# Stick attention in rounds of two heads, attention's norm at eviction, and tokens transposed instead of multiplied with diagonals

## The chip, the cores and the metric

The kernel runs on one core of a Trainium2 chip. The metric is the device time of one launch in microseconds (us), as the median of several runs. The core has TensorE (PE; its weight loads are listed as PEld), VectorE (DVE), ScalarE (ACT), GpSimd (POOL) and SyncE (SP), which run side by side and wait for one another by semaphores; SP starts the loads of the large weights.

## The reference

256 tokens of width 1024 pass through two transformer layers. All is float32.

The first layer: `h = rms_norm(x) * (1 + scale1) + shift1`, where the shifts, scales and gates come from a small network on `c`. Then `proj = h @ w_in` feeds two mixers. The one is banded softmax attention with 8 heads of 64; its output of width 512 is normed over all heads together, `o_a = rms_norm(o_a, attn_out_gain)`, that is, each token is divided by its root mean square. The other is a gated delta rule with 4 heads of 128, `o_b`. Both together give `x = x + gate1 * (concat(o_a, o_b) @ w_out)`. Then `h2 = rms_norm(x) * (1 + scale2) + shift2` goes to PEER: queries `h2 @ w_query`, the best 16 of 128 x 128 experts for each of 8 heads, and `x = x + gate2 * y`.

The second layer: `proj = rms_norm(x) @ w_in_2` is cut into parts for HGRN2 (a gated linear recurrence with 8 heads), for stick-breaking attention with 16 heads of 64, and for two gates. Stick attention, for a block of 128 queries and all keys up to its end, with `z` the scores:

```
log_keep = where(key < query, log_sigmoid(-z), 0)
log_w = log_sigmoid(z) + cumsum(log_keep, reverse) - log_keep
a = where(key < query, exp(log_w), 0);  o = a @ v
```

`mixed = sigmoid(ga) * (o_hg @ w_hg) + sigmoid(gb) * (o_sb @ w_sb)`, `x = x + mixed @ w_o`, and a gated feed-forward layer ends it.

## The kernel before

Tokens lie on partitions in two tiles of 128 (`xt[:, i]`), or, for products that contract over features, transposed: `hT[:, k]` holds features 128k to 128k + 127 of all 256 tokens. Large products are made from two parts of each operand, `hi` (rounded by an ACT copy to float32r) and `lo` (the rest, a subtraction), as three products (`mm3`). Small products in float32 stand in the trace as two records each, a transpose as one. Nearly all rows bear line 237, the one where a helper counts each operation; so groups are told apart by tiles.

*The feeder* (lines 280 to 380) holds the list of weight units, 512 KB each. A unit is loaded by SP into `raw`, split into `whi` (ACT) and `wlo` (DVE, or POOL in some stages), up to three ahead, and multiplied in bursts of a few products. A unit has a gate: it can't start before its `hT` exists. Around it run *chains*, generators that make the mixers step by step. `drive` (line 438) decides in which order the program is written: it keeps an estimate of each engine's time and takes the next chain step when it is ready, else a burst of the feeder. Steps of chains are written with a higher priority (`urgent`), and the framework then orders each engine's instructions by its own simulation, priority and tokens; products that write one PSUM tile, or tiles given one token by `in_order`, keep their order among themselves. Of the 8 PSUM banks, 6 are `acc` and 2 are `tp`.

*Stage a* (line 1111) is the first layer's mixers. `attention_chain` (line 992) ends with the division by the softmax sum into `oa` (which lies in `qa`), then, lines 1079 to 1084, squares on ACT, `rsqrt` (three Newton steps on DVE) and a scaling of both token tiles. After that `split_T` (line 982) transposes `oa` and writes hi and lo into `mT[:, 0:4]`; the delta rule's output `ob` goes to `mT[:, 4:8]` after both of its token tiles are done. The output projection has four accumulators of 128 x 512 (two column halves n, two token tiles i), which stay open over attention's two units and the delta rule's two: `u0[0:2] + u1[0:2]`, later `u0[2:4] + u1[2:4]`. `add_mix` evicts each once: product with `gate1` into `mx_t`, sum into `xt`, squares for the next norm.

*Stage p* (line 1544) is PEER. It starts with `norm_T` (line 610): the sums of squares give `r = 1 / rms`, `norm_diag` makes two diagonal matrices with `r` (`nt_dg`), and `norm_part` (line 546) multiplies each 128 x 128 block of `xt` with one, which transposes and scales at once; DVE then applies scale and shift (`nt_full`), ACT and DVE write hi and lo. The query units start when the first tiles exist, and then the feeder fills PE.

*Stage b* (line 1921) is the second layer. `stick_chain` (line 1807) runs beside the projections of hg, ga, gb and the unit list of w_hg. w_sb's units come next and need its result `sbT`. A bank is 4 heads of equal parity r (the 64 rows r * 64 of `qT` and `kT`), one key block kt and one query block qt. There are 12 banks. `scores` makes `z` and from it on ACT, DVE, ACT, POOL the softplus in hi and lo (`sb_n`, `sb_nr`); `weights` adds the suffix sums to `z` in PSUM by products with `minus`, and takes the exponential (`sb_w`, or `sb_a` for the block 1, 1); `values` multiplies with v into 64 output partitions and evicts them. `sb_n` and `sb_w` take turns in two buffers. The steps are pipelined over banks: scores of bank s, values of bank s - 2, weights of bank s - 1.

## Time and profile before

| | us |
|---|---|
| median of 3 runs (1661.21 to 1662.28) | 1662.23 |
| profiled execution | 1660.82 |
| its span, first to last instruction | 1658.8 |
| PE busy in it | 1604.5 (97%) |
| DVE, ACT, POOL busy | 1094.6, 844.4, 337.3 |
| mean granted clock of PE | 0.988 |

Stage a ends at about 245 us, stage p runs to 1085, stage b to 1460, and the feed-forward layer ends the span. A row of the trace names engine, operation and tiles, `out<-in`; "idle before" is the time for which the engine had nothing to do ahead of an instruction, with what ended it. Matmuls are pipelined, so a record's length is more than the time from one to the next.

### The profile page before, as it was taken

The numbers are of one execution on the slowest core, as the hardware profiler recorded it, in microseconds if no ns is written. First come the engines' busy times: TensorE is split into PE (matmuls) and PEld (weight loads), VectorE is DVE, ScalarE is ACT, GpSimd is POOL, SyncE is SP. The second block draws the span as 40 slices with busy tenths as digits, with TensorE's granted clock in tenths as the row PEclk, the third lists the DMA queues.
The fourth block names the chain that finished last, engine by engine and source line by source line (L and its number), as shares of the span: only waits on it lengthen the run. The fifth ranks groups of instructions, "written<-read, shape, count | busy, mean of one in ns | idle before, by whom it ended". The sixth has DMA issues, their size and how long they took to land.

```text
span 1658.8 us, 28802 instructions
## 1 busy us (share of the span) xinstructions
PE 1604.5 (97%) x11336; PEld 1426.3 (86%) x11336; DVE 1094.6 (66%) x2034; ACT 844.4 (51%) x1314; POOL 337.3 (20%) x277
## 2 busy tenths in 40 slices
PE   7999979998999999999999999999999999999998
PEld 4878757888999999998888888889887898889997
DVE  3874765899967777874444444489886544656555
ACT  4553545654544444455544554465554866454443
POOL 0000001254323222242222222105322201000000
PEclk9999989999999999999999999999999999999999
DMA  8762335444555555556666666653444443546664
GB/s 331 253 218 102 126 110 195 145 153 150 172 164 165 166 166 166 166 166 191 193 195 195 190 193 195 196 155 118 147 125 130 139 141 115 167 141 189 186 185 138
DMA packets 77896, 279.36 MB, mean 168 GB/s; under 512 B 9664, under 2 KB 10048, under 8 KB 77632
## 3 DMA queue, kind: packets, MB, share of 16 engines
q1 hardware_dynamic: 71136, 257.72, 50.6%
q10 hardware_dynamic: 6624, 19.80, 3.6%
q8 instruction: 88, 1.44, 0.4%
q14 instruction: 48, 0.39, 0.1%
HBM read 276.44 MB, written 1.05 MB: 167 GB/s over the span
## 4 chain that ended last, share of the span: by engine, by line
PE 75%; DVE 7%; ACT 1%; issue 1%; POOL 1%; DMA 0%; DVEq 0%; ACTq 0%
PE acc L237 70%; PE tp L237 5%; DVE wlo L237 2%; DVE hg_Z L237 1%; DVE b_f L237 1%; DVE q_v L237 1%; DVE q_i L237 1%; DVE q_oh L237 0%; POOL wlo L237 0%; ACT whi L237 0%; POOL hg_Z L237 0%; DVE b_k L237 0%; DVE q_sc L237 0%; DVE xt L237 0%; ACT hg_Z L237 0%
## 5 line engine op out<-in xcount | busy, mean ns | idle before, releaser
L237 DVE TENSOR_TENSOR wlo<-raw,whi 128x1024 fp32r<-128x1024 f32 x415 | 517.7, 1249 | 371.9 <-ACT whi L237 370.8
L237 ACT ACTIVATE whi<-raw 128x1024 fp32r<-128x1024 f32 x470 | 495.2, 1055 | 407.2 <-PE acc L237 316.4
L237 PE MATMUL acc<-hT_hi,wlo 128*128 128x256 f32 x1728 | 492.8, 286 | 9.6 <-DVE wlo L237 7.8
L237 PE MATMUL acc<-hT_hi,whi 128*128 128x256 f32 x1728 | 494.4, 287 | 2.1 <-ACT whi L237 1.6
L237 PE MATMUL acc<-hT_lo,whi 128*128 128x256 f32 x1728 | 492.1, 285 | 1.3 <-DVE hT_lo L237 1.2
L237 PEld LDWEIGHTS acc<-hT_hi,wlo 128*128 128x128 f32 x1728 | 333.3, 193 | 13.6 <-DVE wlo L237 9.3
L237 PEld LDWEIGHTS acc<-hT_hi,whi 128*128 128x128 f32 x1728 | 333.0, 193 | 6.3 <-ACT whi L237 2.0
L237 PEld LDWEIGHTS acc<-hT_lo,whi 128*128 128x128 f32 x1728 | 333.4, 193 | 3.6 <-DVE hT_lo L237 1.9
L237 PE MATMUL acc<-wlo,hT_hi 128*128 128x512 f32 x832 | 328.1, 395 | 2.0 <-DVE wlo L237 2.0
L237 PE MATMUL acc<-whi,hT_lo 128*128 128x512 f32 x832 | 323.9, 391 | 0.0
L237 PE MATMUL acc<-whi,hT_hi 128*128 128x512 f32 x832 | 261.7, 394 | 0.9 <-ACT hT_hi L237 0.9
L237 POOL TENSOR_TENSOR wlo<-raw,whi 128x1024 fp32r<-128x1024 f32 x55 | 142.4, 2589 | 394.7 <-ACT whi L237 369.0
L237 PEld LDWEIGHTS acc<-wlo,hT_hi 128*128 128x128 f32 x832 | 156.4, 188 | 36.8 <-DVE wlo L237 2.6
L237 PEld LDWEIGHTS acc<-whi,hT_hi 128*128 128x128 f32 x832 | 156.0, 188 | 35.5 <-issue 3.1
L237 PEld LDWEIGHTS acc<-whi,hT_lo 128*128 128x128 f32 x832 | 156.4, 188 | 32.8 <-issue 0.8
L237 POOL TENSOR_TENSOR hT_lo<-A,hT_hi 128x256 fp32r<-128x256 f32 x128 | 97.4, 764 | 241.4 <-ACT hT_hi L237 241.4
L237 ACT ACTIVATE hT_hi<-A 128x256 fp32r<-128x256 f32 x128 | 52.8, 417 | 160.2 <-PE acc L237 160.2
L237 DVE TENSOR_TENSOR oh<-oh1e,c_g 128x512 f16<-128x512 f16 x128 | 75.0, 626 | 10.2 <-PE tp L237 9.5
L237 POOL TENSOR_TENSOR hg_Z<-b_k 128x512 f32<-128x512 f32 (+1 forms) x26 | 38.9, 1523 | 89.2 <-DVE b_k L237 41.9
L237 DVE SCALAR_TENSOR_TENSOR A<-tp,A 128x512 f32<-128x512 f32 (+26 forms) x52 | 28.4, 546 | 27.9 <-PE tp L237 27.8
L237 DVE TENSOR_TENSOR oh1e<-c_ih,iota 128x512 f16<-128x512 f16 x64 | 43.7, 683 | 0.9
L237 POOL TENSOR_TENSOR sb_nr<-sb_n,sb_nr 128x512 fp32r<-128x512 f32 x12 | 19.5, 1626 | 120.4 <-ACT sb_nr L237 120.4
(398 smaller groups left out, 1820.3 us busy)
## 6 DMA issues: line engine op xcount, KB each, us to landing
raw<-in_down SPq DMA_DIRECT2D x128, 512.0 KB, 3.6
raw<-in_up SPq DMA_DIRECT2D x128, 512.0 KB, 3.7
raw<-in_w_in SPq DMA_DIRECT2D x100, 512.0 KB, 3.7
raw<-in_w_ffn_in SPq DMA_DIRECT2D x44, 512.0 KB, 4.3
...
```

Source lines behind the costliest of these rows:

```text
L237: r = f(*args, **kw)
```

## The change

Three edits, and what they need:

- Stick attention goes by rounds: both parities r of 4 heads at a time, 6 rounds instead of 12 banks. Their score products alternate between the two 64-row halves, and their value products between the two halves of the output partitions, which are then evicted together. The order is now: weights of round s - 1, values of round s - 1, scores of round s.
- Attention's 1 / rms is no longer multiplied into `oa`. It is a column factor `ra` in an eviction of attention's part of the output projection, which has its own accumulators now (`tok_units` gets a first block `k0`); the delta rule's part has others, evicted later. `out_chain` transposes each token tile of `ob` as it is done. Attention's scores get a common token.
- `norm_part` scales 128 x 256 blocks of tokens, one on ACT and one on DVE, and transposes them.

```diff
@@ -473,25 +473,26 @@
     return tile
 
 
-def tok_units(g, w, grp, gate, post, ps_of=None, nk=NK):
+def tok_units(g, w, grp, gate, post, k0=0, nk=NK):
+
 
     nc, st = g.nc, []
 
     def unit(kq):
         def fn(wt):
             if kq == 0:
-                st.extend((ps_of or g.ps_acc).tile([128, 512], F32, name="acc") for _ in range(2))
+                st.extend(g.ps_acc.tile([128, 512], F32, name="acc") for _ in range(2))
             for kk in range(2):
                 k = kq * 2 + kk
                 for i in range(2):
-                    mm3(g, st[i], gate[0][:, k, i * 128:(i + 1) * 128], wt[:, kk], k == 0, k == nk - 1)
+                    mm3(g, st[i], gate[0][:, k0 + k, i * 128:(i + 1) * 128], wt[:, kk], k == 0, k == nk - 1)
                     yield
             if kq == nk // 2 - 1:
                 with urgent(g):
                     post(st)
         return fn
 
-    return [(w[grp, kq], (2, 512), unit(kq), gate) for kq in range(nk // 2)]
+    return [(w[grp, k0 // 2 + kq], (2, 512), unit(kq), gate) for kq in range(nk // 2)]
 
 
 def feat_units(g, w, grp, gate, post):
@@ -531,28 +532,37 @@
     g.nc.scalar.activation(junk, x, AF.Square, accum_out=ss)
 
 
+def norm_rms(g, pool, ss):
+
+    s2 = pool.tile([128, 2], F32, name="nt_s2")
+    g.nc.vector.tensor_tensor(s2, ss[:, :, 0], ss[:, :, 1], op=ALU.add)
+    return rsqrt(g, pool, s2, 2, 1.0 / D)
+
+
 def norm_diag(g, pool, ss):
 
-    nc = g.nc
-    s2 = pool.tile([128, 2], F32, name="nt_s2")
-    nc.vector.tensor_tensor(s2, ss[:, :, 0], ss[:, :, 1], op=ALU.add)
-    r = rsqrt(g, pool, s2, 2, 1.0 / D)
+    r = norm_rms(g, pool, ss)
     dg = pool.tile([128, 2, 128], F32, name="nt_dg")
     for i in range(2):
-        nc.vector.tensor_scalar(dg[:, i], g.c["ident"], r[:, i:i + 1], None, op0=ALU.mult)
+        g.nc.vector.tensor_scalar(dg[:, i], g.c["ident"], r[:, i:i + 1], None, op0=ALU.mult)
     return dg, r
 
 
-def norm_part(g, pool, xt, dg, hT, k, n, scale, shift):
-
+def norm_part(g, pool, xt, r, hT, k, scale, shift):
 
     nc = g.nc
-    ps = g.ps_t.tile([128, n, S], F32, name="tp")
-    for kk in range(n):
+    ps = g.ps_t.tile([128, 2, S], F32, name="tp")
+    xs = pool.tile([128, 2, 256], F32, name="nt_xs", tag="q_raw", bufs=8)
+    for i in range(2):
+        x = xt[:, i, k * 128:(k + 2) * 128]
+        if i:
+            nc.vector.tensor_scalar(xs[:, i], x, r[:, i:i + 1], None, op0=ALU.mult)
+        else:
+            nc.scalar.activation(xs[:, i], x, AF.Copy, scale=r[:, i:i + 1])
+    for kk in range(2):
         for i in range(2):
-            mm(g, ps[:, kk, i * 128:(i + 1) * 128], lhsT=xt[:, i, (k + kk) * 128:(k + kk + 1) * 128],
-                             rhs=dg[:, i])
-    for kk in range(n):
+            transpose(g, ps[:, kk, i * 128:(i + 1) * 128], xs[:, i, kk * 128:(kk + 1) * 128])
+    for kk in range(2):
         c = slice(k + kk, k + kk + 1)
         full = pool.tile([128, S], F32, name="nt_full", bufs=2)
         nc.vector.tensor_scalar(full, ps[:, kk], scale[:, c], shift[:, c], op0=ALU.mult, op1=ALU.add)
@@ -610,12 +620,12 @@
 def norm_T(g, pool, xt, ss, scale, shift, gate, n):
 
     with urgent(g):
-        dg, _ = norm_diag(g, pool, ss)
+        r = norm_rms(g, pool, ss)
     hT = hT_tiles(g)
     gate.append(hT)
     for k in range(0, NK, 2):
         with urgent(g):
-            norm_part(g, pool, xt, dg, hT, k, 2, scale, shift)
+            norm_part(g, pool, xt, r, hT, k, scale, shift)
         if k >= 2:
             for _ in range(n):
                 g.fd.burst()
@@ -961,6 +971,10 @@
     for i in range(2):
         yield from need(g, st, "z", f"o{i}")
         delta_out_norm(g, pool, st["o"][:, i], st["z"][:, i], st["rq"][:, i])
+        while "mT" not in st:
+            yield None
+        yield ready_in(g, st["o"][:, i])
+        split_T(g, lambda h: st["o"][:, i, h], lambda f: st["dog"], st["mT"], 4, slice(i * 128, (i + 1) * 128))
         yield 0
 
 
@@ -1026,7 +1040,7 @@
 
     def scores(i, hq):
         n = 128 * (i + 1)
-        sps = [g.ps_acc.tile([128, 2, n], F32, name="acc") for _ in range(2)]
+        sps = [in_order(g, f"at_s{i}{hq}", g.ps_acc.tile([128, 2, n], F32, name="acc")) for _ in range(2)]
         for j in range(2):
             for r in range(2):
                 pr = slice(r * 64, r * 64 + 64)
@@ -1076,13 +1090,6 @@
                 nc.vector.tensor_tensor(oa[:, i].rearrange("p (h d) -> p h d", h=8), o_ps[i], bc(rs[:, i], 2, 64),
                                         op=ALU.mult)
         yield 0
-    s2 = pool.tile([128, 2], F32, name="on_s2")
-    for i in range(2):
-        square_sums(g, pool, oa[:, i], s2[:, i:i + 1])
-    r = rsqrt(g, pool, s2, 2, 1.0 / 512)
-    for i in range(2):
-        nc.vector.tensor_scalar(oa[:, i], oa[:, i], r[:, i:i + 1], None, op0=ALU.mult)
-    yield 0
 
 
 def conv_steps(g, y, x, grp):
@@ -1179,7 +1186,7 @@
             g.c.update({n: ct[:, j] for j, n in enumerate(CNAMES[3:nA])})
             g.convw = sm[:, 0:48].rearrange("p (f t) -> p f t", t=4)
             g.dtb, g.ealog = sm[:, 48:52], sm[:, 52:56]
-            aog, dog = sm[:, 59:63], sm[:, 63:64]
+            aog, st["dog"] = sm[:, 59:63], sm[:, 63:64]
             abw = p1.tile([128, NK, 8], F32, name="abw")
             nc.scalar.dma_start(abw, a.w_ab)
             abs_ = Split(p1.tile([128, NK, 8], F32R, name="abh"), p1.tile([128, NK, 8], F32R, name="abl"))
@@ -1263,32 +1270,39 @@
         g.dump("oa", oa)
         mT = hT_tiles(g)
         wgate.append(mT)
-        with urgent(g):
+        s2 = pool.tile([128, 2], F32, name="on_s2")
+        with urgent(g, 900):
             for i in range(2):
                 split_T(g, lambda h: oa[:, i, h * 128:(h + 1) * 128], lambda f: aog[:, f:f + 1], mT, 0,
                         slice(i * 128, (i + 1) * 128))
+            for i in range(2):
+                square_sums(g, pool, oa[:, i], s2[:, i:i + 1])
+            ra = rsqrt(g, pool, s2, 2, 1.0 / 512)
+        st["mT"] = mT
         ss = g.keep.tile([128, 2, 2], F32, name="nt_ss2")
 
-        def add_mix(n):
+
+        def add_mix(n, attn):
             def post(ps):
                 for i in range(2):
                     sl = slice(n * 512, (n + 1) * 512)
                     t = pool.tile([128, 512], F32, name="mx_t", tag="at_s", bufs=3)
-                    nc.vector.tensor_tensor(t, ps[i], gate1[:, sl], op=ALU.mult)
+                    if attn:
+                        nc.vector.scalar_tensor_tensor(t, ps[i], ra[:, i:i + 1], gate1[:, sl], op0=ALU.mult, op1=ALU.mult)
+                    else:
+                        nc.vector.tensor_tensor(t, ps[i], gate1[:, sl], op=ALU.mult)
                     nc.vector.tensor_tensor(xt[:, i, sl], xt[:, i, sl], t, op=ALU.add)
-                    square_sums(g, pool, xt[:, i, sl], ss[:, i, n:n + 1])
+                    if not attn:
+                        square_sums(g, pool, xt[:, i, sl], ss[:, i, n:n + 1])
             return post
 
-        u0, u1 = (tok_units(g, a.w_out, n, wgate, add_mix(n)) for n in range(2))
-        add_units(g, u0[0:2] + u1[0:2])
+        for n in range(2):
+            add_units(g, tok_units(g, a.w_out, n, wgate, add_mix(n, True), 0, 4))
         drive(g, chains, None, outc)
-        ob = st["o"]
-        g.dump("ob", ob)
+        g.dump("ob", st["o"])
         g.mark("a.onorm")
-        add_units(g, u0[2:4] + u1[2:4])
-        with urgent(g):
-            for i in range(2):
-                split_T(g, lambda h: ob[:, i, h], lambda f: dog, mT, 4, slice(i * 128, (i + 1) * 128))
+        for n in range(2):
+            add_units(g, tok_units(g, a.w_out, n, wgate, add_mix(n, False), 4, 4))
         drive(g, chains, fill=False)
         g.dump("mod2", g.mod2)
         g.mark("a.wout")
@@ -1833,60 +1847,71 @@
             yield 0
     yield from need(g, st.have, "sv0", "sv1")
     sbT = Split(st.tile("sbT_hi"), st.tile("sbT_lo"))
-    banks = [(p0, r, *kq) for p0 in (0, 4) for r in range(2) for kq in ((1, 1), (0, 1), (0, 0))]
+    rounds = [(p0, *kq) for p0 in (0, 4) for kq in ((1, 1), (0, 1), (0, 0))]
+    R2 = range(2)
     T = {}
     a11 = pool.tile([128, 2, 4, 128], F32, name="sb_a", tag="rst")
 
+
     def scores(b):
-        p0, r, kt, qt = b
-        pr = slice(r * 64, r * 64 + 64)
-        z = g.ps_acc.tile([128, 4, 128], F32, name="acc")
+        p0, kt, qt = b
+        zs = [in_order(g, f"sb_z{p0}{kt}{qt}", g.ps_acc.tile([128, 4, 128], F32, name="acc")) for _ in R2]
         if kt == qt:
-            mm(g, z, lhsT=g.ident_r, rhs=bc(g.later, 1, 4), start=True, stop=False)
+            for z in zs:
+                mm(g, z, lhsT=g.ident_r, rhs=bc(g.later, 1, 4), start=True, stop=False)
         for j in range(4):
-            mm(g, z[:, j], lhsT=kT[pr, p0 + j, kt * 128:(kt + 1) * 128], rhs=qT[pr, p0 + j, qt * 128:(qt + 1) * 128],
-               start=kt != qt and j == 0, stop=j == 3)
-        n = pool.tile([128, 4, 128], F32, name="sb_n", tag="sb_s", bufs=2)
-        nc.scalar.activation(n, z, AF.Abs)
-        nc.scalar.activation(n, n, AF.Exp, scale=-1.0)
-        nc.scalar.activation(n, n, AF.Ln, bias=1.0)
-        nc.vector.scalar_tensor_tensor(n, z, 0.0, n, op0=ALU.max, op1=ALU.add)
-        nr = pool.tile([128, 2, 4, 128], F32R, name="sb_nr", tag="hg_Z", bufs=4)
-        nr = Split(nr[:, 0], nr[:, 1])
-        nc.scalar.activation(nr.hi, n, AF.Copy)
-        nc.gpsimd.tensor_tensor(nr.lo, n, nr.hi, op=ALU.subtract)
-        T[b] = [z, nr]
+            for r in R2:
+                pr = slice(r * 64, r * 64 + 64)
+                mm(g, zs[r][:, j], lhsT=kT[pr, p0 + j, kt * 128:(kt + 1) * 128],
+                   rhs=qT[pr, p0 + j, qt * 128:(qt + 1) * 128], start=kt != qt and j == 0, stop=j == 3)
+        T[b] = []
+        for z in zs:
+            n = pool.tile([128, 4, 128], F32, name="sb_n", tag="sb_s", bufs=2)
+            nc.scalar.activation(n, z, AF.Abs)
+            nc.scalar.activation(n, n, AF.Exp, scale=-1.0)
+            nc.scalar.activation(n, n, AF.Ln, bias=1.0)
+            nc.vector.scalar_tensor_tensor(n, z, 0.0, n, op0=ALU.max, op1=ALU.add)
+            nr = pool.tile([128, 2, 4, 128], F32R, name="sb_nr", tag="hg_Z", bufs=4)
+            nr = Split(nr[:, 0], nr[:, 1])
+            nc.scalar.activation(nr.hi, n, AF.Copy)
+            nc.gpsimd.tensor_tensor(nr.lo, n, nr.hi, op=ALU.subtract)
+            T[b].append([z, nr])
 
     def weights(b):
-        p0, r, kt, qt = b
-        z, n = T[b]
-        w = a11[:, r] if kt else pool.tile([128, 4, 128], F32, name="sb_w", tag="sb_s", bufs=2)
-        T[b].append(w)
-        for m, x, last in [(0, n, kt == qt)] + ([] if kt == qt else [(1, T[p0, r, 1, 1][1], True)]):
-            mm(g, z, lhsT=g.minus[:, m], rhs=x.hi, start=False, stop=False, skip_group_check=True)
-            mm(g, z, lhsT=g.minus[:, m], rhs=x.lo, start=False, stop=last, skip_group_check=True)
-        nc.scalar.activation(w, z, AF.Exp)
+        p0, kt, qt = b
+        for r in R2:
+            z, n = T[b][r]
+            w = a11[:, r] if kt else pool.tile([128, 4, 128], F32, name="sb_w", tag="sb_s", bufs=2)
+            T[b][r].append(w)
+            for m, x, last in [(0, n, kt == qt)] + ([] if kt == qt else [(1, T[p0, 1, 1][r][1], True)]):
+                mm(g, z, lhsT=g.minus[:, m], rhs=x.hi, start=False, stop=False, skip_group_check=True)
+                mm(g, z, lhsT=g.minus[:, m], rhs=x.lo, start=False, stop=last, skip_group_check=True)
+            nc.scalar.activation(w, z, AF.Exp)
 
     def values(b):
-        p0, r, kt, qt = b
+        p0, kt, qt = b
         if kt == 1:
             return
-        pr = slice(r * 64, r * 64 + 64)
         ps = g.ps_t.tile([128, 4, 128], F32, name="tp")
         for j in range(4):
-            h = (p0 + j) * 2 + r
-            v = st.have[f"sv{h // 8}"][:, :, h % 8 * 64:h % 8 * 64 + 64]
-            mm(g, ps[pr, j], lhsT=v[:, 0], rhs=T[b][2][:, j], start=True, stop=qt == 0)
-            if qt:
-                mm(g, ps[pr, j], lhsT=v[:, 1], rhs=T[p0, r, 1, 1][2][:, j], start=False, stop=True)
-        ix = (pr, slice(p0, p0 + 4), slice(qt * 128, qt * 128 + 128))
-        split_to(g, sbT.hi[ix], sbT.lo[ix], ps[pr])
-
-    for s in range(len(banks) + 2):
-        for back, f in ((0, scores), (2, values), (1, weights)):
-            if 0 <= s - back < len(banks):
-                f(banks[s - back])
-                yield 0
+            h = (p0 + j) * 2
+            v = st.have[f"sv{h // 8}"]
+            for t in range(1 + qt):
+                for r in R2:
+                    w = T[p0, 1, 1][r][2] if t else T[b][r][2]
+                    mm(g, ps[r * 64:r * 64 + 64, j], lhsT=v[:, t, (h + r) % 8 * 64:(h + r) % 8 * 64 + 64], rhs=w[:, j],
+                       start=t == 0, stop=t == qt)
+        ix = (slice(None), slice(p0, p0 + 4), slice(qt * 128, qt * 128 + 128))
+        split_to(g, sbT.hi[ix], sbT.lo[ix], ps)
+
+    for s in range(len(rounds) + 1):
+        if s:
+            weights(rounds[s - 1])
+            yield 0
+            values(rounds[s - 1])
+        if s < len(rounds):
+            scores(rounds[s])
+            yield 0
     gate.append(sbT)
 
 
```

## Rows read from the trace of the kernel before

**Rows 1.** PE's own waits, 200 to 270 us: total us, times, longest

```profile
PE tp L237 <- DVE nt_dg L237: 7.2, 1, 7.2
PE tp L237 <- DVE qa L237: 5.0, 1, 5.0
```

**Rows 2.** stretches: PE, PEld, DVE, ACT, POOL busy, PE's clock, DMA share, GB/s

```profile
207.00:245.00 38.00, 28.86 (x140) 23.43 (x140) 25.17 (x60) 17.15 (x35) 0.00 (x0) 0.86 0.34 103
...
216.00:242.00 26.00, 25.38 (x127) 20.10 (x125) 16.75 (x31) 14.04 (x28) 0.00 (x0) 0.97 0.40 121
...
245.00:263.00 18.00, 13.45 (x75) 11.22 (x76) 11.15 (x35) 5.67 (x12) 0.00 (x0) 0.82 0.51 160
...
1280.00:1419.00 139.00, 138.32 (x980) 124.29 (x980) 72.14 (x98) 97.17 (x156) 24.80 (x16) 1.00 0.43 130
```

**Rows 3.** timeline of 203 to 224 us: start, length, engine, instruction, idle before

```profile
209.53 0.69 DVE L237 TENSOR_TENSOR qa<-acc,at_rs 128x512 f32<-128x512 f32 x1 [1.33 <-PE acc L237]
...
213.85 0.88 DVE L237 TENSOR_SCALAR qa<-qa,rs_y 128x512 f32<-128x512 f32 x2
...
214.49 1.94 PE L237 MATMUL tp<-consts,qa 128*128 128x128 f32 x8 [4.99 <-DVE qa L237]
...
216.08 0.78 PE L237 MATMUL acc<-whi,hT_hi 128*128 128x512 f32 x1
```

**Rows 4.** groups of DVE's instructions, 208 to 246 us

```profile
L237 DVE TENSOR_TENSOR xt<-xt,mx_t 128x512 f32<-128x512 f32 x4 | 2.6, 684 | 0.0
L237 DVE TENSOR_TENSOR mx_t<-acc,gate 128x512 f32<-128x512 f32 x4 | 2.6, 683 | 0.0
```

**Rows 5.** timeline of 239 to 263 us

```profile
248.15 0.48 DVE L237 TENSOR_SCALAR nt_dg<-consts,rs_y 128x128 f32<-128x128 f32 x2
...
248.59 3.46 PE L237 MATMUL tp<-nt_dg,xt 128*128 128x128 f32 x16 [7.21 <-DVE nt_dg L237]
...
251.87 1.00 DVE L237 TENSOR_SCALAR nt_full<-tp,mod 128x256 f32<-128x256 f32 x2 [3.23 <-PE tp L237]
...
253.90 0.48 PE L237 MATMUL acc<-whi,hT_hi 128*128 128x512 f32 x1
```

**Rows 6.** tiles b_kT and b_sv, 1279 to 1420 us: ns min/median/max

```profile
L237 PE MATMUL acc<-b_qT,b_kT x96: 272/272/373, 1279.9 to 1400.5; 64*128 64x128 f32 x96
...
L237 PE MATMUL tp<-sb_w,b_sv x64: 272/273/323, 1312.3 to 1417.0; 128*64 128x128 f32 x64
L237 PE MATMUL tp<-sb_a,b_sv x32: 272/273/323, 1312.6 to 1415.4; 128*64 128x128 f32 x32
```

**Rows 7.** PE's timeline around 1280, 1189, 1196 and 1218 us

```profile
1279.94 1.16 PE L237 MATMUL acc<-b_qT,b_kT 64*128 64x128 f32 x8
...
1189.03 1.16 PE L237 MATMUL tp<-b_hi,hg_kT 64*128 64x128 f32 x16
...
1195.98 1.09 PE L237 MATMUL acc<-hg_S,b_f 128*64 128x128 f32 x8
...
1218.26 0.66 PE L237 MATMUL acc<-hg_S,b_f 128*64 128x128 f32 x8
```

**Rows 8.** groups of instructions, 1280 to 1419 us

```profile
L237 POOL TENSOR_TENSOR sb_nr<-sb_n,sb_nr 128x512 fp32r<-128x512 f32 x12 | 19.5, 1626 | 120.4 <-ACT sb_nr L237 120.4
L237 ACT ACTIVATE sb_n<-sb_n 128x512 f32<-128x512 f32 x24 | 14.8, 630 | 0.3
L237 DVE SCALAR_TENSOR_TENSOR sb_n<-acc,sb_n 128x512 f32<-128x512 f32 x12 | 8.2, 689 | 11.9 <-ACT sb_n L237 11.9
```

**Rows 9.** PE's own waits, 1280 to 1420 us

```profile
PE acc L237 <- ACT b_sbT_hi L237: 0.7, 1, 0.7
```

**Rows 10.** slices of 1 us, columns as in Rows 2

```profile
217.00:218.00 1.00, 1.00 (x5) 0.74 (x4) 0.82 (x4) 0.68 (x4) 0.00 (x0) 0.76 0.00 0
...
1088.00:1089.00 1.00, 0.57 (x2) 0.57 (x3) 1.00 (x3) 0.59 (x2) 0.00 (x0) 0.50 0.70 238
```

**Rows 11.** PE's timeline of 1080 to 1101 us

```profile
1085.19 1.38 PE L237 MATMUL tp<-consts,xt 128*128 128x128 f32 x8 [1.58 <-DVE xt L237]
```

## The prediction

> **What bounds the kernel now.** I read the stretches first, then PE's waits, then the timeline at each wait, then the tiles that the diff touches.
>
> The stretches [rows 2] show two regimes. From 1280 to 1419 us, where stick attention runs, PE is busy for 138.3 of 139 us: a microsecond of PE work taken out there is a microsecond of the span, as long as something else is ready. From 207 to 263 us PE is busy for 28.9 of 38 and 13.5 of 18 us, and its clock is below full: there the length is set by waits. The two longest of these [rows 1] are 5.0 us on `qa` (end of attention) and 7.2 us on `nt_dg` (start of the PEER stage). The change touches both places and the stick stretch. All else is the same code, so I cost these three; that the build orders other work anew is left to the range.
>
> **Attention's 1 / rms.** Now `qa` is written by the softmax division at 209.53 for 0.69 us, then come squares, a sum, the Newton steps and two scalings that start at 213.85, and PE's transposes start at 214.49 after 4.99 us of idleness [rows 3]. With the scaling moved to the eviction, the transposes need the division alone, done at 210.22; with the hand-over between engines they start at about 210.5, so some 1.0 us of idleness is left and 4.0 us go. What is late next is the first hi and lo tile of mT: products began 1.6 us after the first transpose [rows 3], and tokens 0 to 127, ready earlier, can fill a part of that. Bounds: 5.0 us if they fill all of it, 0 if the chain before is as late as the squares were.
>
> The price is on DVE. The output projection gets a second eviction: four more scaled copies and four more sums, each at the nearest rows' 0.683 and 0.684 us [rows 4], 5.5 us; the sum and Newton steps that stood between the division and the scaling, at most 3.6 us (210.22 to 213.85 [rows 3]), now lie in this stretch too. From 216 to 242 DVE is busy for 16.75 of 26 us [rows 2]; with 5.5 + 3.6 it would be 25.9 of 26. DVE also splits the weights that PE waits for, and the evictions have priority. So I don't cost them at nothing: 1.5 us, between 0 (they fit) and 5.5 (none does). The delta rule's transposes come earlier and by halves; they were not waited for [rows 1], so 0, from -0.5 to +0.5 us. The weights' loads keep queue and order, so no DMA moves. Attention's scores keep their products; the common token only fixes an order: 0.
>
> **Tokens scaled and transposed.** Now: two diagonals (0.48 us from 248.15), then 16 records for the eight products of the first two tiles, 3.46 us at low clock, and `nt_full` can start at 251.87 only [rows 5]. A transpose is one record where such a product is two: eight transposes took 1.94 us, at low clock as well [rows 3]. The scalings, one on ACT and one on DVE, stand in the place of the diagonals; neither is in the trace at this shape, so each is put between 0.24 (half the elements, `nt_dg`) and 0.50 us (the same elements, `nt_full`) [rows 5]: at most 0.3 us more than now. So the first two tiles are ready 3.46 - 1.94 - 0.3 = 1.2 us earlier. The other eight products become transposes beside the query products, where PE is busy, and save about half of a product each at full clock, some 1.0 us. Against it stand four scalings on DVE, 1.0 to 2.0 us beside its own `nt_full` and lo tiles, which PE can wait for. I take -2.0 us; bounds -3.0 (DVE hides its part) and +1.0 (it hides nothing, and PE saves nothing later).
>
> A rule that speaks against this edit: the Trainium skill, "TensorE: Matmul & The Clock Gate", Part 4, says that transposes don't count as TensorE activity in the way products do, and the clock stays low. The trace is divided: after eight transposes and a few products the clock rose within the slice 217 to 218 us [rows 10], but after eight transposes at 1085.19 [rows 11] it fell and is 0.50 in the slice from 1088 [rows 10]. What it would cost is the second rival.
>
> **Stick attention in rounds.** The trace has 96 records of scores and 64 + 32 of values [rows 6], two for each product. Eight records of one bank's scores take 1.16 us, and sixteen records of the same shape (64 rows, 128 columns), which alternate between the upper and lower 64 rows, take 1.16 us too [rows 7]: the halves run at the same time. The rounds put the two heads' scores in just that alternation. Twelve groups of 1.16 become six: -7.0 us; without the ends, where a group overlaps its neighbours, rather -5.5. For values the halves are of output partitions: eight records of 128 rows and 64 columns took 1.09 us in one half and 0.66 in alternation [rows 7], so 12 x 0.43 = -5.2 us. Masks and weights keep their products. That is 10.7 to 12.2; some groups will be cut by other work put between, so I take -10.5 us; bounds -12.2 and 0. Evictions fall from eight on 64 partitions to four on 128, off PE's path.
>
> The change adds a wait here: a round's weights wait for both banks' scores, and the next round's scores for this round's values, since `sb_n` and `sb_w` share two buffers. By the groups' means [rows 8], a round is 1.2 (scores) + 2 x (4 x 0.63 + 0.69) on ACT and DVE + 1.6 on POOL, 9.2 us, then 2 exponentials at 0.63, values at most 4 x 0.66, eviction 0.63 + 0.69: 14.4 us, an estimate without the weights' own products. Six rounds need 86 us; the chain now has 137 us, from 1279.9 to the last values at 1417 [rows 6]. Queued behind its instructions on PE are the projections of ga, gb and hg, which don't need it; only w_sb does. PE waited for its end for 0.7 us [rows 9], so it is nearly late already, and must come 10 us earlier: 21 us for a round, beside the weights' splits on ACT.
>
> **Sum.** -4.0 + 1.5 - 2.0 - 10.5 = -15.0 us. The profiled execution took 1660.82 us (1658.8 of span, 2.0 around it), so 1645.8; the runs' median is 1.4 us above the profiled one: 1662.2 - 15.0 = 1647.2, rounded to 1647.
>
> **Rivals**, all against the median.
> - *The chain of rounds becomes the bound, or the halves don't pair*: the stick ends where it ends now and PE idles for what it saved, or other work is put between the two heads' products so that they run singly. For it: 0.7 us of slack [rows 9] and three serial stages in a round. Against it: 14 us of need where 21 are to be had. Price 10.5: 1657.7, still faster. Chance 0.20 with its partial forms.
> - *The clock stays low after transposes*, by the rule above. Its mechanism here: the first query products run at half clock for as long as the diagonal products did, 3.46 us [rows 5], and lose half of it, 1.7 us: 1648.9. Chance 0.12.
> - *Rounds longer than the banks were.* The other side: place, the buffers of `sb_n` and `sb_w`; if each round takes 25 us (every stage waiting behind ACT's splits and projections on PE), the stick ends at 1279.9 + 150 = 1430, 12 us later than now, and w_sb with it. Less 4.5 from the other edits: 1662.2 + 12 - 4.5 = 1669.7. It decides from 137 / 6 + 4.5 / 6 = 23.6 us a round on. Chance 0.09.
> - The forecast: 0.59.
>
> **How the numbers follow.** A measurement of this kernel can tell 0.2% (3.3 us) from no change. The forecast, the clock's rival and nearly all of the first are faster by more: 0.59 + 0.12 + 0.15 = 0.86; 0.05 of the first, with milder costs on DVE, is within; 0.09 is slower. The forecast's own range is 1641 (all bounds but one at their better ends) to 1653 (half of the pairs, DVE at 3 us). To leave no more than 2 in 10 out, the range takes in the first rival up to 1659: 1641 to 1659.
>
> **What would show it.** Right: PE's wait on `qa` at 1.5 us or less; groups of 16 score records in about 1.2 us; the stretch from the first scores to the first product after the last sbT tile shorter by about 10 us with PE busy all along; eight records before the first `nt_full`, about 1 us sooner after the Newton steps. Wrong: PE waiting for `b_sbT_hi`, `sb_w` or `sb_nr` for microseconds (first or third rival); score records 0.11 us apart without a partner; waits on `wlo` between 211 and 240 us (DVE); a clock of 0.5 for longer in the PEER stage's start.

## The result, and the profile after

The changed kernel took 1640.68 us (median of 4 runs, 1638.98 to 1641.87) where the kernel before took 1661.72 (1658.62 to 1662.28): a ratio of 0.9879 [0.9867, 0.9891]. Timed twice more beside the experiments it took 1640.00 and 1638.69 us, ratios 0.9865 [0.985, 0.988] and 0.9861 [0.9847, 0.9876]; the mean of the three ratios is 0.9868, or 21.9 us. Faster was forecast, but 15 us of it: the three medians lie 0.3, 1.0 and 2.3 us under the lower end of the range, 1641 us. The profiled execution of before (1660.82 us) lay about 1 us under the medians, so the traces have 20.5 us to explain (spans of 1658.8, and 1638.3 by the mean of three).

To see where the 21.9 us come from, I cut the span at five events that every version has. The table is worked out from the starts of instructions in the traces; in it are all kernels that this text speaks of (`full_again` and `full_third` are the changed kernel). The third column ends at the first product with the experts' down weights, the fifth at the first product of w_o.

```
kernel              first attn   to PE's first   to first      to first     to w_o's  to the
                    scores at    norm product    expert(down)  xt transp.   first     end
before                 169.38        79.20          63.35        773.26      348.80   224.77
after                  171.83        72.85          62.05        773.25      335.05   224.99
full_again             172.91        72.84          61.88        770.96      336.00   223.60
full_third             169.71        72.94          62.40        772.63      335.45   223.61
e1_banks               169.79        72.85          62.21        773.76      347.32   223.55
e2_attn_norm_back      171.97        78.75          62.57        771.74      337.76   224.77
e3_diagonals           172.69        72.82          65.51        772.93      338.55   223.56
e4_one_by_one          172.54        72.92          61.79        774.42      340.17   223.54
e5_rounds_alone        173.74        78.64          63.41        771.88      337.41   222.08
e6_pool_splits         169.26        75.35          60.49        772.87      339.10   224.72
e7_warm                171.53        74.23          60.28        771.85      337.85   224.85
e10_late_splits        171.90        71.58          62.56        775.18      337.78   224.70
e11_late_warm          169.15        71.66          60.39        772.40      339.78   224.67
e12_before_warm        169.93        79.86          65.74        773.05      347.94   223.55
```

Two things are to be read before any difference. The first, fourth and sixth columns hold code that no experiment touches, and they move by 4.6, 4.2 and 2.9 us from trace to trace: that is what one trace can't tell. The second column repeats within 0.6 us where the code is the same, so there a single trace tells more; the third repeats within 0.8 us with transposes (leaving out the four runs with moved splits or added products), but with diagonals it moves by 2.4 us. The changed kernel's gain stands in the second column (-6.3), the third (-1.2 by the mean of its three traces) and the fifth (-13.3 by the mean).

**Attention's end.** PE's waits from 200 to 270 us, after [rows 1]; the wait on `qa` has no row any more, and the one before the norm is longer:

```profile
PE tp L237 <- ACT nt_xs L237: 8.9, 1, 8.9
```

The stretches after [rows 2], with the same columns. The first runs from the last values to the last evictions, as 207 to 245 did, in 34 us instead of 38 and with a clock of 0.98 instead of 0.86; DVE's load rose from 25.17 of 38 to 29.89 of 34. The third is stick attention from its first scores to its last values: PE is busy for all of the 113 us.

```profile
207.00:241.00 34.00, 28.62 (x156) 23.08 (x156) 29.89 (x78) 19.30 (x40) 0.00 (x0) 0.98 0.43 126
241.00:259.00 18.00, 14.00 (x66) 10.08 (x66) 13.27 (x38) 7.41 (x16) 0.00 (x0) 0.74 0.62 204
1276.00:1389.00 113.00, 113.00 (x873) 101.97 (x873) 62.51 (x82) 86.57 (x146) 25.01 (x16) 1.00 0.46 136
```

PE's timeline after, where [rows 3] had the wait: tokens 0 to 127 of `qa` are transposed before the last values, projection products fill from 209.64, and the transposes of the second half come 1.0 us after the division of those tokens (on DVE from 211.55 for 0.68 us), with products in between:

```profile
207.53 1.11 PE L237 MATMUL acc<-va,at_pT 128*128 128x64 f32 x8
...
208.58 0.60 PE L237 MATMUL tp<-consts,qa 128*128 128x128 f32 x4
...
209.64 0.51 PE L237 MATMUL acc<-whi,hT_hi 128*128 128x512 f32 x1
...
210.45 1.00 PE L237 MATMUL acc<-va,at_pT 128*128 128x64 f32 x8
211.26 0.48 PE L237 MATMUL acc<-whi,hT_hi 128*128 128x512 f32 x1
...
212.04 0.40 PE L237 MATMUL acc<-whi,hT_hi 128*128 128x512 f32 x1
...
213.19 0.60 PE L237 MATMUL tp<-consts,qa 128*128 128x128 f32 x4
213.63 0.60 PE L237 MATMUL tp<-consts,ob 128*128 128x128 f32 x4
```

PE's own account of the second column, the kernel before and then the changed one (length, PE busy, its clock, DMA share, GB/s). PE sat idle for 13.3 us before and for 9.4 us after, and the same 413 records in between kept it at work for 65.9 us before and 63.4 after (the view counts the first one behind them as well):

```profile
169.38:248.59 79.20, 65.91 (x414) 0.91 0.39 123
171.83:244.68 72.85, 63.41 (x414) 0.97 0.43 131
```

DVE's evictions [rows 4], after, 208 to 246 us: twice as many, and the kind with the scale takes 746 ns:

```profile
L237 DVE TENSOR_TENSOR xt<-xt,mx_t 128x512 f32<-128x512 f32 x8 | 5.4, 683 | 0.0
L237 DVE SCALAR_TENSOR_TENSOR mx_t<-acc,rs_y,gate 128x512 f32<-128x512 f32 x4 | 3.0, 746 | 0.3 <-PE acc L237 0.2
L237 DVE TENSOR_TENSOR mx_t<-acc,gate 128x512 f32<-128x512 f32 x4 | 2.6, 684 | 1.0 <-PE acc L237 1.0
```

**The norm.** DVE's timeline after, answering to [rows 5]. Two splits of query weights (`wlo`) stand among the last additions, ahead of the norm's sum; the scaled tokens `nt_xs` take the diagonals' place, and `nt_full` starts 1.15 us after PE does (3.28 before):

```profile
237.41 0.68 DVE L237 TENSOR_TENSOR xt<-xt,mx_t 128x512 f32<-128x512 f32 x1
238.00 1.22 DVE L237 TENSOR_TENSOR wlo<-raw,whi 128x1024 fp32r<-128x1024 f32 x1
239.14 1.29 DVE L237 TENSOR_TENSOR xt<-xt,mx_t 128x512 f32<-128x512 f32 x2
240.34 1.22 DVE L237 TENSOR_TENSOR wlo<-raw,whi 128x1024 fp32r<-128x1024 f32 x1
241.48 0.15 DVE L237 TENSOR_TENSOR nt_s<-nt_ss 128x2 f32<-128x2 f32 x1
...
244.12 1.14 DVE L237 TENSOR_SCALAR nt_xs<-xt,rs_y 128x256 f32<-128x256 f32 x4
245.83 0.99 DVE L237 TENSOR_SCALAR nt_full<-tp,mod 128x256 f32<-128x256 f32 x2 [0.57 <-PE tp L237]
```

PE's timeline there, after:

```profile
244.68 1.97 PE L237 MATMUL tp<-consts,nt_xs 128*128 128x128 f32 x8 [8.89 <-ACT nt_xs L237]
```

**Stick attention.** Tiles `b_kT` and `sb_w`, after [rows 6]: the same 96 and 64 records, but the last values come at 1387 instead of 1417:

```profile
L237 PE MATMUL acc<-b_qT,b_kT x96: 271/272/375, 1275.9 to 1367.2; 64*128 64x128 f32 x96
...
L237 PE MATMUL tp<-sb_w,b_sv x64: 272/273/324, 1319.0 to 1387.2; 128*64 128x128 f32 x64
```

PE's timeline after, inside three rounds. The halves do pair, as [rows 7] led one to expect: 14 score records in the 1.16 us that 8 took, 12 in 0.94, and four value records in 0.39 us where the kernel before put two in 0.38 (next fence):

```profile
1291.61 0.94 PE L237 MATMUL acc<-b_qT,b_kT 64*128 64x128 f32 x12
...
1306.12 1.16 PE L237 MATMUL acc<-b_qT,b_kT 64*128 64x128 f32 x14
...
1319.31 0.39 PE L237 MATMUL tp<-sb_a,b_sv 128*64 128x128 f32 x4
```

Two rows of the kernel before, PE's timeline: values in stick attention, and attention's last values, which took 1.97 us where the changed kernel needs 1.00 to 1.11:

```profile
1312.59 0.38 PE L237 MATMUL tp<-sb_a,b_sv 128*64 128x128 f32 x2
...
207.52 1.97 PE L237 MATMUL acc<-va,at_pT 128*128 128x64 f32 x8 [0.75 <-ACT at_pT L237]
```

From 1275 to 1420 us PE has no wait on another engine's tile in the changed kernel; the 0.7 us of [rows 9] is gone.

### The profile page after: what moved, and what is told of

It is laid out like the page before. It is cut to its first block, busy times and chain, and to the rows that moved or that the text cites. A ratio compares the mean times of both kernels' runs of the same rounds, so it can differ in the third digit from the quotient of the medians.

```text
span 1640.0 us, 28770 instructions
## 1 busy us (share of the span) xinstructions
PE 1593.3 (97%) x11320; PEld 1415.5 (86%) x11320; DVE 1091.7 (67%) x2038; ACT 841.5 (51%) x1314; POOL 333.9 (20%) x277
## 4 chain that ended last, share of the span: by engine, by line
PE 73%; DVE 9%; issue 1%; ACT 1%; POOL 1%; DMA 0%; DVEq 0%; ACTq 0%
PE acc L237 68%; PE tp L237 5%; DVE wlo L237 2%; DVE q_oh L237 1%; POOL hg_Z L237 1%; DVE b_f L237 1%; DVE q_v L237 1%; ACT whi L237 1%; DVE q_i L237 1%; DVE q_hk L237 0%; DVE b_k L237 0%; DVE oh L237 0%; DVE hg_Z L237 0%; DVE q_pos L237 0%; DMA raw<-in_down 0%
## 5 line engine op out<-in xcount | busy, mean ns | idle before, releaser
L237 DVE TENSOR_TENSOR oh<-oh1e,c_g 128x512 f16<-128x512 f16 x128 | 77.1, 642 | 10.9 <-PE tp L237 10.1
L237 ACT ACTIVATE A<-tp 128x512 f32<-128x512 f32 (+26 forms) x43 | 17.3, 419 | 44.4 <-DVE A L237 40.5
L237 POOL TENSOR_TENSOR sb_nr<-sb_n,sb_nr 128x512 fp32r<-128x512 f32 x12 | 18.6, 1567 | 102.4 <-ACT sb_nr L237 102.4
```

The source lines that it names most:

```text
L237: r = f(*args, **kw)
```

## The experiments

Each edit is against the changed kernel unless the text says otherwise. An interval of a ratio is some 0.15% to either side (2.5 us), so differences between experiments are read from the table's columns first.

**The rounds taken back.** `stick_chain` as before, one bank at a time; the rest is the changed kernel.

```diff
-    rounds = [(p0, *kq) for p0 in (0, 4) for kq in ((1, 1), (0, 1), (0, 0))]
+    banks = [(p0, r, *kq) for p0 in (0, 4) for r in range(2) for kq in ((1, 1), (0, 1), (0, 0))]
...
-    for s in range(len(rounds) + 1):
+    for s in range(len(banks) + 2):
```

> The changed kernel with the 12 banks of before in stick attention; the other two edits stay. My theory: the second layer's mixers shrank from 348.8 us (first transposes to w_o's first product) to 335.1 because the two heads' products share PE's time; so this goes back up by 13.7 us, to 1654, ratio to before 0.995 to 0.997, with 96 score records 0.11 us apart and PE never waiting. Rival: part of the 13.7 us came from another order of everything in that stage (idle time fell by 2.2 us, a stretch at half clock near 1136 us went away), and the banks cost only what PE's own records show, 9.7 us: 1650, ratio 0.993.

Measured: 1650.81 us, 0.9929 [0.9914, 0.9944], 10.1 us above the mean ratio of the changed kernel: the rival's size, not the theory's 13.7. The fifth column goes from 335.5 to 347.3; the others stay.

**Attention taken back.** The scaling by 1 / rms before the transposes, one eviction for each half of the output columns, the delta rule's transposes at the end, and attention's scores without their common token.

```diff
...
+    r = rsqrt(g, pool, s2, 2, 1.0 / 512)
+    for i in range(2):
+        nc.vector.tensor_scalar(oa[:, i], oa[:, i], r[:, i:i + 1], None, op0=ALU.mult)
...
-                        nc.vector.scalar_tensor_tensor(t, ps[i], ra[:, i:i + 1], gate1[:, sl], op0=ALU.mult, op1=ALU.mult)
...
```

> The changed kernel with attention's 1 / rms multiplied into its output again, one accumulator over both halves of the output projection, and the delta rule's output transposed at its end, as before. My theory: the wait of 5.0 us comes back, and with it the low clock around it (2.6 us), less 1.7 us that the wait for the next norm is shorter: up by 6 us, to 1646.5, ratio 0.991. Rival, my forecast's size: 2.5 us (4.0 of waiting less 1.5 of crowding on DVE), 1643, ratio 0.989.

Measured: 1649.35 us, 0.9924 [0.9911, 0.9938], 9.3 us above. The second column is 78.75, so 5.9 us belong to this part. All of its terms come back: PE waits 4.99 us on `qa` and 0.75 us on `at_pT`, the wait before the norm falls from 8.9 to 7.3 us, and the 413 records of this column take 65.3 us of work instead of 63.4. The edit takes back several things at once, so which of them ended the wait on `at_pT` is not shown. 2.3 us more stand in the fifth column, where nothing was edited (see the order of instructions, below).

**The diagonals taken back.**

```diff
-            transpose(g, ps[:, kk, i * 128:(i + 1) * 128], xs[:, i, kk * 128:(kk + 1) * 128])
+            mm(g, ps[:, kk, i * 128:(i + 1) * 128], lhsT=xt[:, i, (k + kk) * 128:(k + kk + 1) * 128],
+                             rhs=dg[:, i])
```

> The changed kernel with the diagonal products of before at the start of PEER; the other two edits stay. The edit's own part in the traces is 1.3 us from PE's first product there to the first product of the expert scores. My theory: it gains 1.7 us of PE time and 1.2 us of waiting, but gives back half of it because the clock stayed at half until 5.5 us after PE resumed, not 3.0: this kernel takes 1 to 2 us more, 1642, and its clock rises about 3 us after the first diagonal product. Rival (transposes keep the clock low and eat the whole gain): 1640 or less, no change or better.

Measured: 1647.76 us, 0.9913 [0.9897, 0.9928], 7.5 us above, more than either expectation; 3.4 of it in the third column, 3.1 in the fifth. PE's clock after the wait is what the rival was about. Stretches of the kernel with diagonals (columns: PE busy, clock, DMA share, GB/s):

```profile
245.00:249.00 4.00, 3.50 (x16) 0.50 0.87 280
249.00:254.00 5.00, 4.25 (x18) 0.50 0.37 152
254.00:256.00 2.00, 2.00 (x16) 0.88 0.12 35
```

and of the changed kernel, where PE resumes at 244.68 with transposes:

```profile
248.00:250.00 2.00, 2.00 (x9) 0.50 0.82 336
250.00:253.00 3.00, 3.00 (x22) 0.96 0.47 108
```

With products instead of transposes PE ran at 1.2 GHz (the half clock, 0.50 in these rows) for 9 us after it resumed at 245.50; with transposes for 5.5 us. In the kernel before, with products, it was 3 us. So the half clock lasts as long or longer without transposes, and they are not what holds it down here.

**Rounds without alternation.** The same rounds and banks, but one head's four products after the other's, for scores and for values.

```diff
-        for j in range(4):
-            for r in R2:
+        for r in R2:
+            for j in range(4):
...
-        for j in range(4):
+        for r, j in [(r, j) for r in R2 for j in range(4)]:
...
```

> The changed kernel, rounds kept, but within a round the score products of the first head's parity stand before those of the second, and so do the value products: the same products, steps, buffers and evictions, without the alternation. My theory (the halves of the array run at the same time only in alternation): PE's time for scores and values goes back from 16.5 to about 26 us, 9.7 us more: 1650, ratio 0.993, records without partners 0.11 us apart. Rival (the rounds themselves, with half as many steps and evictions, made the gain): 1641, as the changed kernel.

Measured: 1644.58 us, 0.9893 [0.9877, 0.9908], 4.2 us above; from the first stick scores to w_o 143.40 us instead of 139.15. The alternation is worth 4.3 us there, not 9.7. PE's timeline of this kernel shows why: its 16 score records in sequence take 1.71 us, not twice 1.16, because the second head's first products begin beside the first head's last ones.

```profile
1308.00 1.71 PE L237 MATMUL acc<-b_qT,b_kT 64*128 64x128 f32 x16
```

Time on PE from each record's start to the next, over the stage, by kind (before; rounds without alternation; after): scores 13.8, 11.8, 9.6 us; values 12.4, 10.6, 6.9. Bringing both heads into one round gives 2.0 + 1.8, the alternation 2.2 + 3.7; without alternation PE's other records took 1.6 us less in this stretch, so it is only 4.3 us longer.

**The changed kernel again**, twice.

> The changed kernel unaltered, for a second trace and ratio in the same session as the others. All theories: 1640.7 us (1639 to 1642), a ratio of 0.9875; the wait before PE's first product of the norm 8.9 us, PE at half clock again where it resumes after that wait. If the half clock after the attention scores of the kernel before was only chance, it may show in this trace too, and the time is then up to 2.6 us more.

> The changed kernel unaltered, beside the next three on the same chip. All theories: 1640 to 1641 us, a ratio of 0.9870; a wait of 8.9 us before the norm's transposes, 72.85 us from the first attention scores to them.

Measured: the ratios at the head of this text; second column 72.84 and 72.94, wait before the norm 8.9 us in both, no half clock at attention's end in any of the changed kernel's traces.

**The rounds alone**, in the kernel before.

> The kernel before with the stick rounds alone; attention's 1 / rms and the norm as they were. Theory (the three parts add up, and the rounds are worth what their removal cost from the changed kernel, 8.3 to 10.1 us): 1661.7 - 9.2 = 1652.5 us (1651 to 1654). Rival (the rounds are worth the whole difference of the stretch between stage b's transposes and w_o, 13.7 us, and the other two parts partly do the same work twice): 1648 us. Rival (the rounds gain only together with the earlier parts, since the planner's placing is the same): 1657 us or more.

Measured: 1650.06 us, 0.9938 [0.9925, 0.9952], which is 10.3 us under the kernel before; fifth column 337.41, 11.4 us less. The parts add up: 10.3 with the rest absent, 10.1 with it present (11.4 and 11.8 by the fifth column). The 13.7 us of the rival are not the rounds'.

**Two splits on GpSimd.**

```diff
+        if self.split in getattr(self, "pool_at", ()):
+            nc.gpsimd.tensor_tensor(lo, raw, hi, op=ALU.subtract)
+            return
...
+        fd.pool_at = (len(fd.units) + 1, len(fd.units) + 2)
```

> The changed kernel with the low parts of two w_query weight splits computed on GpSimd instead of VectorE, so that VectorE goes from attention's last evictions straight to the norm's sum. Theory (the wait before the norm grew because two 1.22 us splits stand between the evictions and the norm on VectorE): the wait falls from 8.9 to about 6.5 us and the time by 2.4 us, to 1638.3 us. Rival (GpSimd's splits are slower, and the weights are then late for the query products; or the other releaser, ScalarE's half of the squares, sets the wait): the wait stays over 8 us, the time within 1 us of 1640.7 or above it.

Measured: 1643.55 us, 0.9889 [0.9874, 0.9904]. The wait grew to 11.3 us: the opposite of what the theory expected. The rival's bounds hold, but not by either of its reasons: VectorE's additions became longer. Its timeline in this kernel, and GpSimd's group of the tile `wlo`:

```profile
233.11 1.89 DVE L237 TENSOR_TENSOR mx_t<-acc,gate 128x512 f32<-128x512 f32 x3 [1.03 <-PE acc L237]
234.92 5.57 DVE L237 TENSOR_TENSOR xt<-xt,mx_t 128x512 f32<-128x512 f32 x3
```

```profile
L237 POOL TENSOR_TENSOR wlo<-raw,whi x2: 2346/2565/2784, 234.2 to 236.6; 128x1024 fp32r<-128x1024 f32 x2
```

The three additions took 5.57 us (2.22, 2.83 and 0.68, the last of them after GpSimd's work) instead of 1.97. The three evictions just before them, one of whose inputs is a PSUM bank, took 1.89 us as in the changed kernel, although GpSimd had begun at 234.25, before the last of them. The Trainium skill, "SBUF — State Buffer", section "SBUF: two separate sides", says that a VectorE instruction with two SBUF inputs and a GpSimd instruction that reads SBUF exclude each other for a whole instruction; these rows agree.

**Five products in the wait.**

```diff
+        w = g.ps_acc.tile([128, 512], F32, name="acc")
+        for _ in range(5):
+            mm(g, w, lhsT=xt[:, 0, 512:640], rhs=xt[:, 0, 512:1024])
```

> The changed kernel with five extra products (fp32, 128 x 512, into a spare bank) at the start of the norm's transposes; their result is not used. Theory (PE's half clock where it resumes costs some 2 to 2.5 us, and PE is idle there anyway): the extra products run in the wait, the clock is full within a few us of the resumption, and the time falls by 1 to 2.5 us, to 1638.2 to 1639.7 us. Rival (five products of 0.43 us full clock, 0.86 us at half clock, and two passes each, overrun the wait and delay the transposes): 1641.7 to 1645 us. Rival (clock has no price there, DVE and ScalarE set the pace): 1640.7 us.

Measured: 1640.87 us, 0.9871 [0.9856, 0.9886], no change. PE's timeline of this kernel: the products waited 4.1 us for their tokens, then overran the wait,

```profile
239.66 6.26 PE L237 MATMUL acc<-xt 128*128 128x512 f32 x10 [4.09 <-DVE xt L237]
245.76 1.04 PE L237 MATMUL tp<-consts,nt_xs 128*128 128x128 f32 x8
```

so the transposes came 1.4 us later (second column 74.23). They then took 1.04 us, not 1.97, and expert(down) came 0.5 us earlier than in the changed kernel (134.5 us after the first scores; 135.0 by the mean of its three traces) all the same.

**Late splits.** The low parts of those two splits behind the norm's second pair of blocks, on VectorE.

```diff
...
+        if k >= 2 and g.fd.held:
+            lo, raw, hi = g.fd.held.pop(0)
+            one = pool.tile([128, 1], F32, name="nt_one", bufs=2)
+            g.nc.vector.tensor_scalar(one, hT.lo[:, k + 1, 0:1], 0.0, 1.0, op0=ALU.mult, op1=ALU.add)
+            g.nc.vector.scalar_tensor_tensor(lo, raw, one, hi, op0=ALU.mult, op1=ALU.subtract)
...
```

> The changed kernel with the low parts of two w_query weight splits put on VectorE behind the norm's second pair of blocks (they are multiplied with a one made from that pair, so they cannot run sooner). Theory, mended after the run with the splits on GpSimd: only the split at 238.00 stands before a token addition (1.14 us); the one at 240.34 ends within 0.2 us of the squares that the norm waits for anyway. So the wait falls from 8.9 to 7.6 us (7.4 to 7.8) and the stretch by 1.2 us; the splits then cost VectorE up to 2.4 us inside the norm, where it has about 0.9 us to spare in each pair of blocks, so the time moves by -1.2 to 0 us: 1639.4 us. Rival (both splits count, as was first thought): the wait falls to 6.5 us. Rival (VectorE has no room in the norm): the first expert(down) product comes no earlier, and the time is 1640.5 us or more.

**Late splits, and PE kept at work.** As the last, with six products of token columns that are ready early.

```diff
...
+        w = g.ps_acc.tile([128, 512], F32, name="acc")
+        for _ in range(6):
+            mm(g, w, lhsT=xt[:, 0, 0:128], rhs=xt[:, 0, 0:512])
...
```

> As the run with the late splits, and PE kept at work in the wait: six fp32 products of 128 x 512 from token columns that are ready (0.86 us each at full clock, 5.2 us in all, in a wait of about 7.6 us); their result is not used. Theory (the half clock where PE resumes costs 1.8 us, as the run with five late products suggested: its transposes began 1.4 us later and expert(down) all the same 0.4 us earlier): no half-clock stretch between 236 and 250, first expert(down) product 2 to 3 us earlier after the first scores than in the changed kernel (134.9), time 1638 us. Rival (the norm is paced by VectorE and ScalarE, PE's clock does not matter): expert(down) within 0.5 us of the run with the late splits alone.

Measured: 1642.78 us, 0.9880 [0.9865, 0.9895] for the first; 1639.86 us, 0.9867 [0.9853, 0.9882] for the second. PE's wait and stretches of the kernel with late splits,

```profile
PE tp L237 <- ACT nt_xs L237: 7.6, 1, 7.6
```

```profile
240.00:250.00 10.00, 6.20 (x25) 0.50 0.52 171
```

and of the one with products as well:

```profile
PE tp L237 <- ACT nt_xs L237: 2.5, 1, 2.5
```

```profile
241.00:244.00 3.00, 2.67 (x13) 0.50 1.01 412
245.00:255.00 10.00, 10.00 (x57) 1.00 0.69 212
```

The wait fell to the 7.6 us of the theory: one split cost 1.3 us, not two 2.4. Inside the norm the moved splits cost nothing that shows: the third column is 62.56 us with 6.6 us of half clock after PE resumed, and 62.57 us with 6.7 in `e2_attn_norm_back`, which has no moved splits. The first kernel's traced run (1645.47 us) is over the changed one's because its fourth and fifth columns are 2.9 and 2.3 us longer, where its code is the same (for the fifth, see the order of instructions below). With the products, the 10.2 us at 1.2 GHz became 3.4, and from the first scores to expert(down) it took 132.05 us instead of 134.14: 2.1 us go with the shorter half clock at this place, with the splits equal and the transposes at the same point (71.58 and 71.66 us after the first scores). That the clock would not fall at all was wrong. Against the changed kernel (135.0 by the mean of three) the two edits give 2.9 us here, but no time: the fifth column took 4.3 us back (below). No version beat the changed kernel.

**One product in attention's wait**, in the kernel before.

```diff
+    w = g.ps_acc.tile([128, 512], F32, name="acc")
+    mm(g, w[0:2], lhsT=s2, rhs=vt[:, 1])
```

> The kernel before with one extra fp32 product (2 x 512, result unused) that needs the sum of squares of attention's last tokens, so that it runs some 2 us into PE's 5.0 us wait; the eight adaLN products behind it move into the wait with it. Nothing else is changed. Theory (a third of what the changed kernel gained in attention is the clock, which PE lost by thin work around that wait): the half-clock stretch is shorter than the 10.2 or 6.8 us of before, and from the first scores to PE's first product of the norm it is 76.5 to 77.5 us instead of 79.2 (about 0.8 us of that is the adaLN products, which fill the wait instead of later time); time 1659.5 us. Rival (no price of the clock): 78.4 us, all of it the adaLN products; time 1661 us. Rival (the extra products are late and delay the transposes): over 79.2 us.

Measured: 1661.76 us, 1.0002 [0.9992, 1.0012]; second column 79.86. The edit failed at its aim, as this kernel's timeline and stretches show:

```profile
209.56 1.01 PE L237 MATMUL acc<-va,on_s 128*2 128x512 f32 x1 [1.54 <-ACT sqj L237]
...
214.53 1.95 PE L237 MATMUL tp<-consts,qa 128*128 128x128 f32 x8
```

```profile
209.00:214.00 5.00, 3.92 (x20) 0.50 0.13 26
214.00:218.00 4.00, 4.00 (x17) 0.50 0.58 229
218.00:222.00 4.00, 4.00 (x23) 0.96 0.01 4
```

PE had work for 3.9 of the 5 us (adaLN's products moved in behind the added one), and its clock stayed at 1.2 GHz until the stretch from 218, where it is 0.96. The column came out over 79.2 us as in the last rival, but not by its reason: the transposes of `qa` were 0.5 us earlier after the first scores than in the kernel before. PE's idle time in the column fell from 13.3 to 9.4 us, but its work grew from 65.9 to 70.4 us, 1.0 of it the added product. So attention's price of the clock could not be tried by itself; what stands for it is read from rows, below.

**The order of instructions, which no experiment aimed at.** PE's sequence from the first `xt` transposes to w_o differs between versions whose code is the same there. The three traces of the changed kernel agree in all 2298 records. `e2`, `e3`, `e6`, `e7`, `e10` and `e11`, which differ from it only hundreds of microseconds earlier, differ in 452 to 455 positions, `e5` in 454; `before` differs from `e1` in 454. All of these lie ahead of the first stick scores. There are two orders of that part: one in the changed kernel, `e1` and `e4`, the other, but for at most 4 records, in the remaining nine traces, the kernel before among them. With alternating rounds the first took 335.05, 335.45 and 336.00 us in the fifth column, the second 337.41 to 339.78 (seven versions, mean 338.3): 2.8 us, and the ranges don't meet. PE's idle time ahead of the stick scores differs with the order: 3.7 to 4.7 us in the five traces of the first, 5.9 to 6.6 in the nine of the second. A part of the 2.8 us is the clock: of the traces with alternating rounds the two longest, `e6` and `e11`, have 10.2 us of half clock in this column, the first trace of the changed kernel has 3.4 and the rest 6.8. Where it is 6.8, the first order took 335.45 and 336.00 us, the second 337.41 to 338.55 (five versions): 2.1 us. With banks, at 6.8 us as well, it is 1.5 (`e1` against `before`). From the first stick scores to w_o, both orders took 139.15 us, to the hundredth, in all ten traces with alternating rounds, where PE is never without work, and the three with banks 154.05. These 14.9 us are more than the rounds are worth, because with banks fewer of PE's records stand ahead of the first stick scores (1187 against 1205). That the order is the cause was not tried by itself.

## Why the prediction was right, and where its sizes were off

The table sets the steps against the traces; after is the mean of its three.

```
step                                    forecast   measured
attention's wait                          -4.0       -5.0    (5.0 -> 0)
wait on at_pT before the last values       none      -0.8    (0.75 -> 0)
work at attention's end, half clock        none      -2.5    (65.9 -> 63.4)
DVE crowded by the second eviction        +1.5       +1.7    (wait 7.2 -> 8.9)
smaller waits                                        +0.2
  sum of the second column                -2.5       -6.3
norm by transposes                        -2.0       -1.2    (63.35 -> 62.11)
rounds                                   -10.5      -10.5    (348.80 -> 338.3)
order of what stands ahead of the stick     0        -2.8    (338.3 -> 335.5)
start and untouched stretches               0        +0.4    (+2.1, -1.0, -0.7)
  sum                                    -15.0      -20.4
```

- *Attention's wait* was mis-sized by 1.0 us. The forecast left 1 us of idleness for the hand-over and said that tokens 0 to 127 could fill a part; they filled all of it.
- *The half clock* is the larger miss of this column. [Rows 2] showed 0.86 over the stretch, and the forecast priced the wait alone. In the kernel before PE ran at 1.2 GHz from 207.2 to 217.5 us: the last values took 1.97 us (1.00 to 1.11 in the changed kernel), the eight transposes of `qa` 1.59 from the first one's start to the next instruction's (2 x 0.44), the first three products behind them 1.42 (0.78). That is 0.9 + 0.7 + 0.6 = 2.2 us of the 2.5 by which the same 413 records took less work. All three traces with attention as before and nothing in the wait have that stretch (10.2, 6.8 and 6.8 us long, with 65.9, 65.3 and 65.4 us of work), and none of the ten traces with attention as changed. That it costs time is shown at the norm (2.1 us); for attention it is worked out from these rows, and the one run that was to try it alone did not shorten the stretch.
- *The wait on `at_pT`*, 0.75 us before attention's last values, was in the same three traces and in none of the ten. The forecast didn't cost it; what ended it is not shown.
- *DVE's crowding* was right in size and wrong in place. The forecast looked for PE's waits on `wlo` between 211 and 240 us; there are none. The cost came after them, in the wait before the norm, where weights' splits stand between the last additions (with attention taken back that wait is 7.3 us again). One of the splits costs 1.3 us, the late splits show; of the 5.7 us of added evictions and additions (3.0 + 4 x 0.68) hardly more came to light.
- *The norm* was worth 1.2 us against this trace of before, and 3.4 against the diagonals in the changed kernel. The two differ by how long the clock stayed at half after PE resumed: versions with diagonals took 63.35 and 63.41 us where it was 3.0 and 3.4 us, 65.51 and 65.74 where it was 9 and 9.5. The forecast of 2.0 lies between; its step (one record for two) was right. At about equal half clock the edit gives more: 60.49 and 60.39 us with transposes (`e6` and `e11`, 3.5 and 3.4 us) against 63.41 with diagonals (`e5`, 3.4 us), 2.9 us less.
- *The rounds* were right to within the trace-to-trace spread: scores gave 4.2 us (forecast 5.5), values 5.5 (5.2), the masks 0.7; 10.3 us alone and 10.1 taken back by the times, 11.4 and 11.8 by the fifth column. One reason was off: the products pair partly even without the alternation, which is worth 4.3 us of it.
- *The order* was left to the range as something that could not be costed. By the traces it came to 2.8 us, or 2.1 at equal half clock, as much as the forecast gave the norm.

The direction, the three places and the rounds' size were forecast; the sum was not. With every bound at its better end (-5.0, 0, -0.5, -3.0, -12.2) the working gives -20.7 us, 1641.5; so 1641 is not reached with one bound left out, and half of the pairs with DVE at 3 us gives 1654, not 1653. The measured 21.9 us lie beyond all of these bounds together. What carried the time there, the clock at attention's end, the wait on `at_pT` and the order, had no term in the sum, and that it came so near the end of the range is luck.

The rivals. *The chain becomes the bound* fell: PE has no wait there, and the last values come 30 us earlier, so w_sb no longer waits for them. *Rounds too long* fell: six rounds took 111.56 us, 18.6 each, under the 23.6 from which it would decide and over the 14.4 that were estimated. *The clock stays low after transposes* fell in its cause, but not in its price. Its sign came: in the first pair of traces the clock was at half for 5.5 us after PE resumed, where the kernel before had 3.0. By the rule of the Trainium skill ("TensorE: Matmul & The Clock Gate", Part 4) the transposes would be the reason. The traces do not bear that out: the clock was at half for 3.5 to 6.7 us after PE resumed with transposes (eight traces), and for 3.0 to 9.5 us after it resumed with products of diagonals (four). What PE resumes with does not explain the length, and what does was not tried. But the norm gave 1.2 us where it gives 2.9 at equal half clock: by that estimate (`e6` and `e11` hold other edits too) 1.7 us, as much as this rival asked for, went to the longer stretch.

Taking single parts back overstates them here: 10.1 + 9.3 + 7.5 = 26.9 us against 21.9. Two of the three also lost the changed kernel's order, 2.3 and 3.1 us in the fifth column, and without that the sum is 21.5.
